# Eight instead of six of sixteen row tiles in seven products, and the MLP's pairs in another order

## The chip, the cores and the metric

The kernel runs on one core of a Trainium2 chip. The core has a matrix engine (TensorE, PE in the profile, with its weight loads as PEld), a vector engine (VectorE, DVE), a scalar engine (ScalarE, ACT), GpSimd (POOL) and a sync engine (SP) that issues most DMAs. Each engine works through its own instructions in order and waits for others by semaphores. The metric is the device time of one execution in microseconds.

## The reference

Two layers of a streaming encoder over 256 rows of 2048 columns, all in float32. Layer 1 is causal attention with forget gates over 16 heads, layer 2 attention in chunks of 64 with a learned bias on shared keys and values. Behind each attention stands the same MLP with its own weights, 2048 to 8192 to 2048; most of the work is there:

```
def sq_relu_mlp(h, g, w1, w2):
    a = jax.nn.relu(rms_norm(h, g) @ w1)
    return (a * a) @ w2
```

## The kernel before

**Products.** A float32 product is made of three passes on PE (lines 471, 473 and 475): each operand is split into a rounded high part and a low remainder, and high x high, high x low and low x high are summed. The weights come from HBM as tiles of 128 x 1024 (a *unit*: two row tiles of 512 columns), and `issue` (line 219) splits each: ACT writes `hi`, then DVE subtracts it from the tile and writes `lo`. Three `hi`/`lo` buffers of 1024 columns, and one of 512, let the splits run ahead of PE.

**Pairs.** A *pair* is two neighbouring panels of 512 output columns (a and b) over 16 row tiles, for both blocks of 128 rows. Of a part of the row tiles the products are made by Strassen's scheme: seven products in place of eight. The seven weight operands (*forms*) are, in order, 11, T3 = 22 + 12, T2 = T3 + 11, T1 = 12 + 11, 21, T4 = T2 + 21 and 22, where 11, 12, 21 and 22 are blocks of the weights. T3 and T2 are added on DVE (line 824); T1 and T4 are made by DMAs that POOL issues and that add a block from HBM onto a tile in place (line 830). On the side of the activations sums of row tiles stand against them (`S` for the MLP's input, `Sh` for a chunk of hidden columns), made and split in `sums`. A small pair uses four of its sixteen row tiles so, a wide one six: each form is then a unit of 1024 columns (f) and a half unit of 512 (h), with 2 + 1 products of three passes. The other row tiles are *own* units (a3 to a7, b3 to b7), each with four products of three passes. Of the 32 MLP pairs 30 are wide; the first of each MLP and the two pairs of the second layer's query are small.

**Order.** The MLP's 8192 hidden columns go in four chunks. A chunk has two pairs of the first matrix (four panels of hidden columns), then two pairs of the second matrix, which add to the residual. `plan_mlp` writes the order of all units out once, `Pair.plan` that inside a pair: forms, with own units between them, the last three of panel b (b5 to b7) among the first forms of the next pair. Every engine keeps the written order.

**Fill.** Everything else (turning a hidden panel, squaring, sums) is cut into steps in a list of slots. `run_fill` takes one slot after every own unit. A finished hidden panel is transposed in 32 x 32 blocks by DVE, written to DRAM and read back in four pieces by SP (`carry`), and `take` squares and splits it in the slots that a table names.

**Loads.** SP issues the own units' loads, three ahead. The wide blocks are brought by `bring` to rooms of 1536 columns, two each in the tags "k" and "v", at times that the tuple `units` counts in own units before the pair's start, as the adds of T3 and T1.

Of the kernel before, what the change touches and what calls it, by code (L numbers as in the profile page):

```python
# [9 lines left out]
F32 = mybir.dt.float32  # L10
# [5 lines left out]
P = 128  # L16
T = 256
# [11 lines left out]
AHEAD = 2  # L29
EARLY = 3  # L30
UA = UN // 512
REL = 384
WIDE = UN + 512
WIDE1 = (1, 2, 3, 4, 5, 6, 7)
# [15 lines left out]
def trunk(ctx: ExitStack, tc: tile.TileContext, xT, xr, gs, hg, bf, wgate, w_in, w_oa, w1a, w1fa, w1sa, w2fa, w2sa,  # L50
# [24 lines left out]
    def load_x(i):  # L75
        raw_x[i] = qkv.tile([P, WIDE], F32, name="xin", tag="kv"[i // 2], bufs=2)[:, : GH * T].rearrange("p (a t) -> p a t", a=GH)
        if i:
            SY.dma_start(raw_x[i], xT[:, i * GH : (i + 1) * GH, :])
# [40 lines left out]
    class Pair:  # L119
# [3 lines left out]
        def __init__(self, big, src, order, third, units, wide=False):  # L123
            self.big, self.src, self.third, self.units, self.order = big, src, third, units, order
            self.ps, self.t, self.adds, self.wide, self.own = None, {}, order != "early", wide, 3 if wide else 2
# [4 lines left out]
        def plan(self, rest):  # L130
            made = [self.items(f"f{i} h{i}" if self.wide else f"f{i}") for i in range(7)]
            own = {"early": "a2 F a3 F b2 F b3 a4 b4 a5 a6 a7", "wide": "a3 F b3 F a4 F b4 a5 a6 a7", "ahead": "a3 F a4 F a5 F a6 a7 b3 b4",
                   "query": "a2 F b2 F a3 F b3 a4 b4 a5 a6 a7", "": "a2 F a3 F a4 F a5 a6 a7 b2 b3 b4"}[self.order].split()
# [10 lines left out]
    def plan_mlp(w1, w1f, w1s, w2f, w2s, tail, more=None):  # L144
        pairs = []

        def add(w, wf, ws, i, wides, order, when):
            j = wides.index(i) if i in wides else i - sum(1 for k in wides if k < i)
            names = ("11", "12", "21", "22")
            if i in wides:  # L150
                src = [[None] * 3 + [ws[10 * j + 5 * q + u] for u in range(5)] for q in range(2)]
# [4 lines left out]
            pairs.append(Pair(big, src, order, len(pairs) % 2 == 0, when, i in wides))  # L156

        close = (7, 5, 1, 4, 3, 2)
        for c in range(NCH):
            for q in range(2):  # L160
                i = 2 * c + q
                order = "ahead" if i else "early"
                when = (25, 20, 9, 15, 10, 8) if not i else (9, 7, 1, 5, 3, 2) if i == 1 else close
                add(w1, w1f, w1s, i, WIDE1, order, when)
            for q in range(2):
                i = 2 * c + q
                add(None, w2f, w2s, i, WIDE2, "wide", close)
        if more is not None:
            for q in range(2):
                add(more, None, None, q, (), "" if q else "query", close)  # L170
# [910 lines left out]
```

## Time and profile before

| | |
|---|---|
| median of 3 runs | 2086.82 us (2086.47 to 2088.3) |
| span of the profiled execution | 2084.3 us |
| between span and median | 2.5 us |
| PE, DVE, ACT, POOL busy | 100%, 78%, 60%, 6% |
| granted PE clock | 1.00 |
| first MLP | about 350 to 1000 us |
| second MLP | about 1390 to 2080 us |

The profiled execution has no time of its own apart from its span; the median stands 2.5 us over it. A row of the groups view gives line, engine, operation, tiles and count, then the busy time and the mean of one in ns, then the idle time of the engine before them and what ended it. A row of the windows view gives the busy time of each engine in a stretch, the granted clock, the share of time that the 16 DMA engines were busy, and GB/s. A row of the DMA view gives the tiles, the issuing queue, the count, the size and the median time from issue to landing.

### The profile page before, as it was taken

What the parts mean: (1) busy time and instruction counts of PE and PEld (TensorE: products, weight loads), DVE (VectorE), ACT (ScalarE), POOL (GpSimd) and SP (SyncE); (2) the same over time, 40 slices, a digit from 0 to 9 for tenths busy, and PEclk for the clock granted to TensorE, in tenths of its full rate; (3) what the DMA queues carried; (4) which work ended last, traced back from release to release, by engine and by line L of the source; (5) the groups of instructions that cost most, each with busy time, mean ns of one, the idle gap of its engine ahead of it and who ended that gap; (6) DMA issues with size and microseconds to landing.
All of it is one profiled execution on the core that took longest, in us unless ns stands there. A gap on an engine that the chain in (4) does not pass through costs nothing.

```text
span 2084.3 us, 26346 instructions
## 1 busy us (share of the span) xinstructions
PE 2076.9 (100%) x9230; PEld 1721.4 (83%) x9230; DVE 1629.7 (78%) x1964; ACT 1256.1 (60%) x1637; POOL 118.4 (6%) x131
## 2 busy tenths in 40 slices
PE   9999999999999999999999999999999999999999
PEld 7888888888888888888878888888888888888887
DVE  6767666888788888788888677778987887888786
ACT  6544455766566566567676455456765665665664
POOL 1111000000000000000011001000000000000000
PEclk9999999999999999999999999999999999999999
DMA  7787788798798799789988777787987987988895
GB/s 288 247 257 243 225 258 265 253 276 277 235 286 270 251 278 298 217 276 294 269 244 276 225 239 234 244 265 265 282 264 254 278 272 241 289 271 250 271 288 165
DMA packets 181397, 540.93 MB, mean 260 GB/s; under 512 B 36864, under 2 KB 71568, under 8 KB 181264
## 3 DMA queue, kind: packets, MB, share of 16 engines
q1 hardware_dynamic: 170384, 483.60, 68.7%
q0 software_dynamic: 10592, 55.08, 14.3%
q8 instruction: 72, 1.18, 0.2%
q10 hardware_dynamic: 288, 0.57, 0.1%
q14 instruction: 61, 0.50, 0.1%
HBM read 499.30 MB, written 39.87 MB: 259 GB/s over the span
## 4 chain that ended last, share of the span: by engine, by line
PE 98%; DMA 1%; DVE 0%; ACT 0%; issue 0%; ACTq 0%; DVEq 0%; SPq 0%
PE acc L473 26%; PE acc L471 26%; PE acc L475 26%; PE s L471 6%; PE s L473 6%; PE s L475 6%; PE s L614 1%; PE po L644 1%; DMA w<-in_w2fa 0%; PE s L613 0%; PE po L645 0%; DMA raw<-in_w_in 0%; DVE lo L220 0%; ACT hi L219 0%; PE s L737 0%
## 5 line engine op out<-in xcount | busy, mean ns | idle before, releaser
L220 DVE TENSOR_TENSOR lo<-raw,hi 128x1024 fp32r<-128x1024 f32 (+1 forms) x574 | 695.5, 1215 | 219.5 <-ACT hi L219 203.6
L219 ACT ACTIVATE hi<-raw 128x1024 fp32r<-128x1024 f32 (+1 forms) x574 | 602.8, 1051 | 255.6 <-PE acc L473 194.8
L471 PE MATMUL acc<-hi,act 128*128 128x512 f32 x2108 | 580.3, 393 | 1.6 <-ACT hi L219 1.6
L473 PE MATMUL acc<-hi,act 128*128 128x512 f32 x2108 | 571.3, 389 | 0.1
L475 PE MATMUL acc<-lo,act 128*128 128x512 f32 x2108 | 570.9, 389 | 0.0
L473 PEld LDWEIGHTS acc<-hi,act 128*128 128x128 f32 x2108 | 395.5, 188 | 83.2 <-DVE act L311 0.7
L475 PEld LDWEIGHTS acc<-lo,act 128*128 128x128 f32 x2108 | 395.6, 188 | 82.2
L471 PEld LDWEIGHTS acc<-hi,act 128*128 128x128 f32 x2108 | 393.7, 188 | 81.5 <-ACT hi L219 1.7
L219 ACT ACTIVATE hi<-w 128x1024 fp32r<-128x1024 f32 x138 | 145.7, 1056 | 108.1 <-DMA w<-in_w1fa 25.1
L220 DVE TENSOR_TENSOR lo<-w,hi 128x1024 fp32r<-128x1024 f32 x138 | 167.5, 1214 | 27.4 <-ACT hi L219 25.0
L220 DVE TENSOR_TENSOR lo<-wT,hi 128x1024 fp32r<-128x1024 f32 x94 | 114.6, 1219 | 64.0 <-ACT hi L219 64.0
L219 ACT ACTIVATE hih<-w 128x512 fp32r<-128x512 f32 x120 | 75.2, 627 | 76.5 <-PE acc L473 65.5
L219 ACT ACTIVATE hi<-wT 128x1024 fp32r<-128x1024 f32 x94 | 99.1, 1055 | 27.7 <-PE acc L473 9.1
L471 PE MATMUL s<-hi,act 128*128 128x512 f32 x386 | 104.6, 389 | 0.0
L475 PE MATMUL s<-lo,act 128*128 128x512 f32 x386 | 104.6, 389 | 0.0
L473 PE MATMUL s<-hi,act 128*128 128x512 f32 x386 | 104.6, 389 | 0.0
L219 ACT ACTIVATE hih<-wT 128x512 fp32r<-128x512 f32 x90 | 56.4, 627 | 72.9 <-PE acc L473 63.2
L220 DVE TENSOR_TENSOR loh<-w,hih 128x512 fp32r<-128x512 f32 x120 | 82.3, 686 | 18.9 <-ACT hih L219 18.8
L473 PEld LDWEIGHTS s<-hi,act 128*128 128x128 f32 x386 | 72.5, 188 | 15.1
L475 PEld LDWEIGHTS s<-lo,act 128*128 128x128 f32 x386 | 72.5, 188 | 15.0
L471 PEld LDWEIGHTS s<-hi,act 128*128 128x128 f32 x386 | 72.4, 188 | 15.0
L220 DVE TENSOR_TENSOR loh<-wT,hih 128x512 fp32r<-128x512 f32 x90 | 62.0, 689 | 21.0 <-ACT hih L219 20.7
(220 smaller groups left out, 1961.4 us busy)
## 6 DMA issues: line engine op xcount, KB each, us to landing
raw<-in_w_in SPq DMA_DIRECT2D x95, 512.0 KB, 4.5
raw<-in_w2sa SPq DMA_DIRECT2D x80, 512.0 KB, 5.8
raw<-in_w2sb SPq DMA_DIRECT2D x80, 512.0 KB, 5.8
raw<-in_w1sa SPq DMA_DIRECT2D x70, 512.0 KB, 6.0
raw<-in_w1sb SPq DMA_DIRECT2D x70, 512.0 KB, 6.0
raw<-in_w_kv SPq DMA_DIRECT2D x64, 512.0 KB, 4.5
turn<-z SPq DMA_DIRECT2D x60, 512.0 KB, 4.2
w<-in_w2fa SPq DMA_DIRECT2D x32, 768.0 KB, 7.4
```

The costliest lines, as they stand in the source:

```text
L219: S.activation(hi[:, c], raw[:, c], AF.Copy)
L220: V.tensor_tensor(lo[:, c], raw[:, c], hi[:, c].bitcast(F32), op=ALU.subtract)
L471: TE.matmul(ps[:, cols], xh, cut(hi, j), start=first, stop=False, **kw)
L473: TE.matmul(ps[:, cols], xl, cut(hi, j), start=False, stop=False, **kw)
L475: TE.matmul(ps[:, cols], xh, cut(lo, j), start=False, stop=last, **kw)
L614: TE.matmul(s[:, P : 3 * P], q[:, a, P:T], k[:, a], start=True, stop=True)
L644: TE.matmul(po[:, :T], v[:, 0, a * P : (a + 1) * P], pT[:, :2], start=True, stop=False)
```

## The change

- The thirty wide pairs become *deep*: eight of sixteen row tiles go through the seven forms. A form is two units of 1024 columns (f and h), each with two products of three passes; eight own units remain (a4 to a7, b4 to b7). T3 and T2 are added in two halves. The half-width `hi`/`lo` buffers are no longer used by them.
- Four rooms of 2048 columns (k0, k1, v0, v1), one buffer each, take the blocks; each pair passes them on in rotation. The accumulating DMAs are 1024 KB. The scratch for POOL's descriptors is set to 2048 bytes.
- The order of the pairs is new: between the two second-matrix pairs of a chunk, and behind them, stands one first-matrix pair of the next chunk.
- A slot of fill also follows every second unit of a form (`run_fill` in the branch of the forms), and `fetch` is called for each unit of a form.
- Most hidden panels hop: `hop` moves 16 blocks of 32 partitions by DMA from the transposed tile straight to the other tile, eight issued by SP and eight by POOL. In each MLP three of sixteen, the second panel of chunks 1 to 3, still go by `carry`. The tables of slots and times are new.
- `S` and `Sh` hold sums of eight row tiles; tiles in the pool "p" are 4096 instead of 3456 columns.

```diff
+    "deep0": "a4 F F b4 a5 F a6 a7",
+    "deep1": "a4 F b4 F F a5 a6 a7",
+    "ahead0": "F a4 F a5 a6 a7 F b4",
+    "ahead1": "a4 F a5 F a6 a7 F b4",
...
+UNITS = {
+    "W1I1": (9, 7, 6, 5, 4, 1),
+    "W1F": (6, 5, 1, 4, 4, 1),
+    "W1S": (6, 5, 2, 4, 4, 3),
+    "W2F": (7, 5, 1, 5, 4, 3),
+    "W2S": (8, 8, 3, 4, 3, 2),
+    "W2L": (6, 6, 1, 3, 3, 1),
...
+TURNS = (
+    ((1, -1, 4, 5, 6, 6, 6, 9, 9),
+     (0, -1, 3, 5, 7, 7, 8, 9, 9),
+     (1, -1, 5, 7, 7, 7),
+     (1, -1, 3, 4, 5, 5)),
+    ((0, -1, 4, 14, 14, 14, 14, 19, 19),
+     (0, 3, 7, 10, 10, 13, 16, 18, 19),
+     (1, -1, 4, 6, 7, 7),
+     (0, -1, 4, 5, 5, 5)),
+)
...
+DEEP = 2 * UN
...
+        rooms = {"12": "v0", "22": "k0", "11": "k1", "21": "v1"}
+        seq = [(0, 0, 0), (0, 0, 1)]
         for c in range(NCH):
+            seq += [(1, c, 0)] + [(0, c + 1, 0)] * (c + 1 < NCH) + [(1, c, 1)] + [(0, c + 1, 1)] * (c + 1 < NCH)
...
+            p.rooms = rooms
+            if p.adds:
+                rooms = {"12": rooms["11"], "22": rooms["12"], "11": rooms["21"], "21": rooms["22"]}
...
-        if form and half == form.pair.wide:
+        if form and form.pair.deep and form.name == "T3":
+            make(form.pair, "T2", int(half))
+        elif form and half == form.pair.wide:
...
     def room(tag, name, dtype=F32):
-        return qkv.tile([P, WIDE], dtype, name=name, tag=tag, bufs=1 if tag == "bias" else 2)
+        return qkv.tile([P, DEEP], dtype, name=name, tag=tag, bufs=1)
...
+    def hop(z, dst):
+        n = z.shape[1] // 4
+
+        def go():
+            for i in range(4):
+                for j in range(4):
+                    (G if i % 2 else SY).dma_start(dst[32 * j : 32 * j + 32, i * n : (i + 1) * n], z[32 * i : 32 * i + 32, j * n : (j + 1) * n])
+
+        return [[go], [], [], [], []]
...
-    def form_products(ps, hi, lo, x, fs, i, half, stop):
+    def form_products(ps, hi, lo, x, fs, i, half, p):
         items = []
-        for g in (2,) if half else range(2):
+        groups = p.cols // 512
+        for g in range(2, groups) if half else range(2):
...
+        p.t[name] = room(p.rooms[name], "w" + name)
+        SY.dma_start(p.t[name][:, : p.cols], p.big[name])
...
-        G.dma_start(p.t[name][:, : WIDE if p.wide else UN], p.big[other], accum_op=ALU.add)
+        G.dma_start(p.t[name][:, : p.cols], p.big[other], accum_op=ALU.add)
...
     def prepare(p, d):
+        if p.deep and d == p.units[4] - 1:
+            make(p, "T3", 1)
...
-            hi, lo = ready.popleft()[:2] if q > 1 and ready else fetch()
+            hi, lo = ready.popleft()[:2] if q > 1 and ready and not p.deep else fetch()
...
-                    top_up(AHEAD - 1)
+                    if not p.deep:
+                        top_up(AHEAD - 1)
                     if u == 1:
                         S.activation(p.ps[1][0], p.ps[1][1], AF.Copy, scale=-1.0)
+                    if p.deep:
+                        run_fill()
...
-    nc = bacc.Bacc("TRN2", target_bir_lowering=False, num_devices=1)
+    nc = bacc.Bacc("TRN2", target_bir_lowering=False, num_devices=1, dynamic_dma_scratch_size=2048)
```

More of the change, by code (lines that the diff above doesn't have):

```diff
@@ L121, in trunk, with __init__ @@
         fast = True
[L123 to L125 removed]
+        def __init__(self, big, src, order, third, units, wide=UN):
+            self.big, self.src, self.third, self.units = big, src, third, units
+            self.ps, self.t, self.adds, self.order = None, {}, order != "early", order
+            self.deep, self.wide = wide == DEEP, wide > UN
+            self.cols, self.own = wide, wide // 512
         def items(self, names):
@@ L131, in plan @@
             made = [self.items(f"f{i} h{i}" if self.wide else f"f{i}") for i in range(7)]
-            own = {"early": "a2 F a3 F b2 F b3 a4 b4 a5 a6 a7", "wide": "a3 F b3 F a4 F b4 a5 a6 a7", "ahead": "a3 F a4 F a5 F a6 a7 b3 b4",
-                   "query": "a2 F b2 F a3 F b3 a4 b4 a5 a6 a7", "": "a2 F a3 F a4 F a5 a6 a7 b2 b3 b4"}[self.order].split()
+            own = ORDERS[self.order].split()
             plan = made[0] + rest[:1] + made[1] + rest[1:2] + made[2] + rest[2:] + made[3]
@@ L211, in issue @@
             form, half = raw, raw.half
-            raw, cuts = form.pair.t[form.name], [slice(0, 512 if half else UN)]
+            raw, cuts = form.pair.t[form.name], [slice(0, form.pair.cols - UN if half else UN)]
             if half:
@@ L229, in half_next @@
         u = raws[0][0] if raws else units[0]
-        return isinstance(u, Form) and u.half
+        return isinstance(u, Form) and u.half and not u.pair.deep
     def top_up(ahead=AHEAD, early=EARLY):
```

118 lines of the change are left out of this document (63 added, 55 removed), and 3 rows, old and new, of the table ORDERS.

## The prediction

> **What bounds the kernel now.** I read the page first: busy shares, slices, the chain.
>
> ```profile
> span 2084.3 us, 26346 instructions
> PE 2076.9 (100%) x9230; PEld 1721.4 (83%) x9230; DVE 1629.7 (78%) x1964; ACT 1256.1 (60%) x1637; POOL 118.4 (6%) x131
> PE 98%; DMA 1%; DVE 0%; ACT 0%; issue 0%; ACTq 0%; DVEq 0%; SPq 0%
> ```
>
> PE is idle for 7.4 us of 2084.3, and the chain is PE for 98%. What counts is the number of matmuls and whether the other engines still deliver in time. The profiled execution spans 2084.3 us; the median of the runs is 2086.8 us, so 2.5 us lie around the span. I apply differences to the median.
>
> Next the stretches of one pair (about 41 us) by engine, then PE's timeline in plain units, where four matmuls of one pass stand on a line.
>
> ```profile
> 618.00:659.00 41.00, 41.00 (x183) 33.95 (x182) 35.70 (x40) 28.66 (x34) 1.71 (x2) 1.00 0.97 296
> 659.00:700.00 41.00, 41.00 (x183) 33.96 (x182) 32.62 (x34) 22.81 (x27) 1.71 (x2) 1.00 0.77 235
> sum 409.00, PE 409.00 PEld 338.78 DVE 338.02 ACT 262.89 POOL 16.19; mean PE 40.90 PEld 33.88 DVE 33.80 ACT 26.29 POOL 1.62
> 618.00:645.00 27.00, 27.00 (x121) 22.37 (x120) 25.17 (x31) 19.26 (x25) 1.71 (x2) 1.00 0.95 268
> ...
> 944.96 1.07 PE L473 MATMUL acc<-hi,act 128*128 128x512 f32 x4
> 954.02 1.07 PE L475 MATMUL acc<-lo,act 128*128 128x512 f32 x4
> ```
>
> The columns after the stretch are PE, PEld, DVE, ACT and POOL busy, the granted clock (1.00), the DMA share and GB/s; the third row covers ten such stretches (415 to 824 us). PE never waits here. DVE is at 33.8 of 40.9 us, ACT at 26.3. The DMA share swings: 0.97 where hidden panels are turned, 0.77 where only weights move. From 944.96 to 954.02 ten groups of four start, so a matmul costs PE 9.06 / 40 = 0.2265 us.
>
> **The change, part by part.**
>
> *Matmuls removed.* A wide pair issues per form (2 + 1) products of 3 passes, 7 forms: 63 matmuls, and 10 own units of 12: 183. After it, 7 x 4 x 3 = 84 and 8 units of 12: 180. Thirty pairs lose 90 matmuls: 90 x 0.2265 = 20.4 us on the path. A pair then lasts 180 x 0.2265 = 40.8 us, a half form 1.36 us, an own unit 2.72 us.
>
> *Splits and adds.*
>
> ```profile
> L220 DVE TENSOR_TENSOR lo<-raw,hi 128x1024 fp32r<-128x1024 f32 x570 | 692.9, 1219 | 218.5 <-ACT hi L219 202.6 <-PE acc L473 9.3 <-DMA raw<-in_w2sa 1.1
> L219 ACT ACTIVATE hi<-raw 128x1024 fp32r<-128x1024 f32 x570 | 600.5, 1054 | 254.7 <-PE acc L473 194.8 <-PE s L473 18.3 <-DMA raw<-in_w_in 14.0
> L220 DVE TENSOR_TENSOR loh<-w,hih 128x512 fp32r<-128x512 f32 x120 | 82.3, 686 | 18.9 <-ACT hih L219 18.8
> L219 ACT ACTIVATE hih<-w 128x512 fp32r<-128x512 f32 x120 | 75.2, 627 | 76.5 <-PE acc L473 65.5 <-PE s L473 9.9
> L824 DVE TENSOR_TENSOR wT<-wT,w 128x1536 f32<-128x1536 f32 x30 | 52.8, 1759 | 1.0
> L824 DVE TENSOR_TENSOR wT<-w,w 128x1536 f32<-128x1536 f32 x30 | 52.0, 1734 | 0.0
> L296 DVE TENSOR_TENSOR Sh<-sum,Sh 128x512 fp32r<-128x512 f32 x24 | 15.7, 683 | 0.0
> ```
>
> Per pair: full splits go from 17 to 22, half-width ones from 7 to none, and T3 and T2 become two adds of 1024 columns each, which I price like a split. DVE: +5 x 1.219 - 7 x 0.686 - 1.759 - 1.734 + 4 x 1.219 = +2.7 us. ACT: 5 x 1.054 - 7 x 0.627 = +0.9 us, covered by over 10 us idle a pair. The second hidden panel's sums are now full-width: one more low split (0.683) and wider adds, an estimate of 1.3 us a chunk, 0.3 us a pair. DVE's 33.8 of 40.9 becomes 34.2 + 2.7 + 0.3 = 37.2 of 40.8 us, 91% on average. Pairs that handle the first two hidden panels stand higher: 35.7 + 2.7 + 0.6 = 39.0, or 96%. The fourth row of the windows above is the cover: 27 us with DVE busy for 25.17 (93%) and PE never waiting. If 93% were DVE's ceiling, 39.0 would need 41.8 us: 1.0 us of stall in each of 16 such pairs, 16 us. If its gaps there are mere slack, the cost is nothing. I take 4 us, nearer nothing, since the new order puts a second-matrix pair between the heavy ones and single wide adds no longer hold the queue for 1.76 us.
>
> *Lookahead.* Forms are now two equal units of 1.36 us through the three-deep hi/lo buffers. A split starts when PE leaves the hi pass of the unit three back, some 4 us before its low half is needed; ACT and DVE together take 1.05 + 1.22 us plus a hand-over. About 1.5 us of slack remains, which one add of 1.22 us fits. Cost nothing while DVE isn't behind.
>
> *DMA.*
>
> ```profile
> q1 hardware_dynamic: 170384, 483.60, 68.7%
> q0 software_dynamic: 10592, 55.08, 14.3%
> raw<-in_w2sa SPq DMA_DIRECT2D x80, 512.0 KB, 5.8
> turn<-z SPq DMA_DIRECT2D x60, 512.0 KB, 4.2
> w<-in_w2fa SPq DMA_DIRECT2D x32, 768.0 KB, 7.4
> q<-turn SPq DMA_DIRECT2D x168, 128.0 KB, 5.5
> w<-in_w1fa POOLq DMA_DIRECT2D x7, 768.0 KB, 9.7
> wT<-in_w2fb POOLq DMA_DIRECT2D x8, 768.0 KB, 7.8
> pbuf<-turn SPq DMA_DIRECT2D x128, 48.0 KB, 2.8
> query<-in_w_qb POOLq DMA_DIRECT2D x2, 512.0 KB, 5.9
> query<-turn POOLq DMA_DIRECT2D x4, 128.0 KB, 5.2
> L347 POOL DMA_DIRECT2D query<-turn x4: 552/568/612, 1063.7 to 1065.4; - x4
> L347 SPq DMA_DIRECT2D q<-turn x168: 325/426/1282, 345.9 to 2012.6; - x168
> L331 DVE STREAM_TRANSPOSE z<-acc 128x512 f32<-128x512 f32 x48 | 31.4, 692 | 5.1 <-PE acc L475 5.1
> ```
>
> Weights read by plain loads stay 8 MB a pair (4 x 768 + 10 x 512 KB against 4 x 1024 + 8 x 512). Only the two accumulating loads of a pair (T1, T4) grow by a third. Sixty of them are 47 of the queue's 55 MB, so about 12% of 16 engines' span, 4.2 us each, now 5.7: +2.9 us a pair. Turning a panel raises the share by 0.20 over two pairs of 82 us for four panels, 4.1 us of all engines each; 26 of 32 panels now hop from SBUF to SBUF without the write to DRAM. A hop costs between half of that and all of it. Four pairs with four turns then come to (0.77 x 164 + 4 x 2.9 + 10 to 16) / 163 = 0.91 to 0.94 throughout. That is below the 0.97 which PE bears today without waiting, and it no longer swings.
>
> *Queues.* Each hop puts 8 issues on SP and 8 on POOL. On POOL that is 8 x 0.57 = 4.6 us, ahead of which the next pair's T1 may stand and behind which nothing urgent does, T4 having gone before. From the end of the panel: transposes 1.3 us (two of 0.69 us, overlapping), 7 x 0.57 = 4.0 us, landing 5.2 us: 10.5 us. The squared ReLU is asked for four slots on, 10.9 us later. For the last panel of a chunk it is asked for after 8 to 9.5 us, up to 2.5 us early; ACT then waits with two units in hand, mostly an own unit. I take 1 us for all hops; nothing and 8 x 2.5 = 20 us are the ends, and the spare units point to the lower.
>
> *Rooms.* Each wide load now has one room, passed on from pair to pair. Block 22 can be fetched only once T1 of the pair before is split: T1's second half is a unit at 17.7 us, split nearly two units ahead, done at an estimated 15.4 us; where SP first writes out a panel, 18 us. From 512 to 768 KB the landing grows by 1.6 us, so 1 MB takes about 9.0 us and lands at 24.4 to 27.0; T3 is asked for behind the own unit at 24.5 us, so near 25.9 at the earliest. DVE may wait 1.1 us, in front of own units or forms with as much slack. Nothing to 1.1 x 8 = 9 us; I take 0, as every other transition has 1.5 us or more.
>
> *The end and the start* keep their order (the last two second-matrix pairs still follow each other). Nothing.
>
> **Sum:** 2086.8 - 20.4 + 4 + 1 + 0 = 2071.4 us.
>
> **Rivals.**
>
> *T4 lands late: the slower one.* T4 adds block 21 from HBM into T2's room. POOL must wait until T2 is split, then the load runs, and its result is due at the sixth form.
>
> ```profile
> 671.57 0.60 ACT L908 ACTIVATE p<-acc 128x512 f32<-128x512 f32 x1 [3.40 <-PE acc L475]
> 673.01 0.59 ACT L914 ACTIVATE acc<-acc 128x512 f32<-128x512 f32 x1
> 675.27 0.86 POOL L830 DMA_DIRECT2D wT<-in_w2fa  x1 [13.02 <-DVE loh L220]
> POOL wT L830 <- DVE loh L220: 360.4, 29, 14.2
> ```
>
> ACT stands in front of this split until PE ends the second form (8.2 us into the pair); two copies of 0.6 us and the split (1.05 + 1.22 us) put T2's last low half at 11.8 us. In 14 pairs (orders "deep0" and "ahead0") the sixth form's split must start by 23.3 us: 11.5 us for the load. In the other 16 one more own unit lies between: 14.2 us. From 5.9 us (512 KB) and 7.8 us (768 KB) the new one takes 9.7 us, 10.4 in proportion: in time by over a us. But the slowest accumulating row, 9.7 us, in proportion gives 12.9 us, and the gain is gone (14 x 1.4 = 20 us). It decides for slower from 13.3 us (14 x 1.8 = 25 us); at 14 us the time is 2086.8 - 20.4 + 35 = 2101 us. Against it: the 9.7 us row is T1's, issued among many loads, T4's rows are the lower ones, and POOL holds nothing before it.
>
> *DVE is the bound.* At the 93% ceiling above: 16 us in place of 4, and with up to 9 us of late T3 the time is 2082 to 2091 us. It needs heavy pairs to stand 1.5 us over (above 3.3 us of forced gaps a pair) to end slower.
>
> *Small pieces are served one by one.* If a group of four short pieces (2.8 us and three further issues of some 0.42 us, 4.1 us) had to end before the next began, the 16 pieces of a hop would take 16.4 us, 5.5 us beyond the slots; with 1.5 us covered, 26 x 4 = 104 us, or 2170 us. Against it: four 128 KB pieces, in total as much as a hop, land 5.2 to 5.5 us after issue though issued on top of each other. The Trainium skill, DMA: Bandwidth & Descriptors, section Bandwidth, says that transfers under 64 KB are descriptor-dominated and gives 0.95 us for 64 KB and 0.68 us for 4 KB; at an estimate of 0.8 us by that page, sixteen in a row take 13 us, with the transposes 3.4 us late, and 26 x (3.4 - 1.5) = 49 us give 2120 us. The trace's overlapping pieces speak against a plain sum of that kind. No run here shows a 32 KB piece between two SBUF tiles.
>
> **Chances.** The forecast (stalls of 0 to 10 us, 2066 to 2077 us): 0.58. Half the gain eaten by DVE or by T3's waits (2077 to 2082.6): 0.12. Gain and stalls cancel, within 4.2 us, the 0.2% that a measurement can tell: 0.10. Slower 0.20: T4 0.11, hops 0.05, DVE 0.04. So faster 0.70, same 0.10, slower 0.20. The range starts at the full gain and a us beyond, 2065, and ends at 2092 us, which leaves the slower cases out.
>
> **What would show it.** Right: 512-column splits gone, full splits of w and wT 120 and 90 higher, those of raw 60 lower; PE with about 9140 matmuls and still 99% or more; DVE near 37 of 40.8 us; DMA share even, 0.90 to 0.95; accumulating rows near 9 to 10.5 us. Wrong: PE idle in front of forms released by DVE (DVE bound), ACT waiting over 2 us for wT loads (T4) or for q after a hop; more than 20 us of PE idle in all makes the prediction wrong.

## The result, and the profile after

The changed kernel takes 2090.07 us (median of 17 runs, 2084.96 to 2097.05) against 2087.31 us for the kernel before in the same job (17 runs, 2085.26 to 2089.75): a ratio of 1.0014, 95% interval 1.0006 to 1.0022. It is slower by 0.14%, inside the 0.2% that was taken for no change, where a gain of 0.7% was forecast. The forecast was 18.7 us too low; the time lies inside its range.

The page of the profile after the change (span and busy shares, POOL's DMA queue, chain, issues with KB and median us to landing; the last three rows are of the DMA view):

```profile
span 2088.3 us, 26874 instructions
PE 2068.8 (99%) x9140; PEld 1703.1 (82%) x9140; DVE 1710.9 (82%) x1974; ACT 1313.2 (63%) x1587; POOL 224.7 (11%) x339
...
q0 software_dynamic: 17248, 77.64, 18.7%
...
PE 76%; issue 10%; DMA 10%; DVE 3%; ACT 1%; POOL 0%; SPq 0%; ACTq 0%; DVEq 0%; POOLq 0%
wT<-in_w2fa POOLq DMA_DIRECT2D x8, 1024.0 KB, 10.6
q<-z SPq DMA_DIRECT2D x208, 32.0 KB, 5.6
q<-z POOLq DMA_DIRECT2D x208, 32.0 KB, 5.8
```

PE has the 9140 matmuls that the change promised, 90 fewer, yet the chain is PE for only 76%, not 98%. The 4.0 us by which the profiled span grew (2088.3 against 2084.3) split up from the two pages: 90 matmuls fewer, -20.4 us; PE idle for 2088.3 - 2068.8 = 19.5 us in place of 7.4, +12.1 us; and PE busy for 2068.8 us where 2076.9 - 20.4 = 2056.5 would do, +12.3 us. The last is not more work but the same matmuls, taking longer. One stall of the first chunk shows how PE comes to wait. The timelines of POOL, SP, ScalarE (ACT) and PE around it (start, duration, operation, count, and in brackets the idle time before it and what ended that):

```profile
473.85 0.92 POOL L882 DMA_DIRECT2D wT<-in_w2fa  x1 [8.60 <-DVE lo L257]
480.71 3.46 POOL L395 DMA_DIRECT2D q<-z  x7 [5.94 <-DMA w<-in_w1fa]
487.53 0.50 POOL L395 DMA_DIRECT2D q<-z  x1 [3.35 <-DMA q<-z]
...
480.44 7.52 SPq L395 DMA_DIRECT2D q<-z  x8
488.08 0.51 SPq L860 DMA_DIRECT2D w<-in_w1fa  x1
...
487.36 2.00 ACT L256 ACTIVATE hi<-wT 128x1024 fp32r<-128x1024 f32 x2 [6.02 <-DMA wT<-in_w2fa]
...
488.46 0.99 PE L519 MATMUL acc<-hi,act 128*128 128x512 f32 x2 [2.34 <-ACT hi L256]
489.25 1.06 PE L521 MATMUL acc<-hi,act 128*128 128x512 f32 x2
490.11 1.06 PE L523 MATMUL acc<-lo,act 128*128 128x512 f32 x2
```

T4, the load that adds block 21 into T2's room, is issued at 473.85. ScalarE asks for its sum from 481.3 on, waits 6.02 us, gets it at 487.36, and PE stands for 2.34 us. In between a hop is under way: SP needs 7.52 us to issue its eight pieces (the fastest of the 26 hops takes 4.9 us), and POOL gives out seven and must wait 3.35 us for a landing before the eighth. SP's next weight load, at 488.08, stands behind that. The rows of the tile give T4's own landing here and in the same place two chunks later, the next two are POOL's timeline there, and the last shows the granted clock behind the stall (the column ahead of the DMA share):

```profile
DMA to landing us min/median/max: 13.4/13.4/13.4
DMA to landing us min/median/max: 11.6/11.6/11.6
...
808.45 0.92 POOL L882 DMA_DIRECT2D wT<-in_w2fa  x1 [9.42 <-DVE lo L257]
820.30 0.50 POOL L395 DMA_DIRECT2D q<-z  x1 [2.03 <-DMA wT<-in_w2fa]
...
488.80:492.10 3.30, 3.30 (x9) 2.58 (x8) 3.30 (x4) 3.26 (x4) 0.00 (x0) 0.50 0.91 298
```

T4 took 13.4 us here and 11.6 us two chunks later. What POOL's eighth piece waits for can be worked out from these rows: T4 lands at 473.85 + 13.4 = 487.25, and the piece starts at 487.53, 0.28 us later; in the other place T4 lands at 808.45 + 11.6 = 820.05, and the piece starts at 820.30. So it waits for T4, although nothing in the data asks for that. The operands of the issues say why: each names a semaphore that its landing raises, SP and ScalarE take eight of them in turn (100, 102, 104, 105, 106, 108, 109 and 110), POOL eight others (111 to 118), and an issue waits until the transfer issued eight before it has landed. Eight back from a hop's eighth piece on POOL stands the adding load that was issued ahead of the hop. SP's eighth piece, at 487.45, waits in the same way for a weight load issued at 475.07.

Behind the stall PE runs at half its clock: 0.50 is granted from 488.8 to 492.1, and the last two lines of PE's timeline, two matmuls each, start 0.86 us apart, 0.43 us a matmul rather than 0.2265. The trace has this stretch as 3.41 us long, so it costs 1.7 us. The Trainium skill, TensorE: Matmul & The Clock Gate, Part 1, says that the clock halves after an idle window of about 3.4 us; here a stand of 2.34 us came before it, and the page's half rate agrees with the granted 0.50.

Half clock explains only a part of the 12.3 us. The trace has one more such stretch inside the run, 7.5 to 10.9 us, behind the start; the two cost 3.4 us. The other 9 us pass at full clock. The view counts a line as busy until about 0.39 us after its last matmul starts (two last 0.62 us, four 1.07), while the next could start after 0.2265 us, so up to 0.16 us of every delay counts as busy. By the starts in the two traces such hidden delays come to 19.1 us at full clock, before to 10.4.

Over the whole run these are the waits for arriving data that ScalarE and POOL show (total us, times, longest):

```profile
ACT hi L256 <- DMA wT<-in_w2fa: 19.7, 6, 6.0
ACT hi L256 <- DMA wT<-in_w2fb: 8.7, 3, 4.2
ACT q L899 <- DMA q<-z: 5.4, 4, 2.0
POOL q L395 <- DMA q<-z: 28.1, 11, 4.1
```

The first two are the accumulating loads of the second matrix, 28.4 us over 9 waits. The third is the squared ReLU that asks for a panel before it has landed. The fourth is new in kind: pieces of a hop held on POOL. The view names the landing it saw last, here a piece; by the operands five of these waits, 18.4 of the 28.1 us, are for T1 or T4 as in the first place above, and six are for an earlier piece of the same hop, where T1 was issued between the pieces. Further holds by T1 and T4 stand in rows under their own names.

### The profile page after: what moved, and what is told of

The parts are those of the page before. It is cut to its first block, busy times and chain, and to the rows that moved or that the text cites. A ratio compares the mean times of both kernels' runs of the same rounds, so it can differ in the third digit from the quotient of the medians.

```text
span 2088.3 us, 26874 instructions
## 1 busy us (share of the span) xinstructions
PE 2068.8 (99%) x9140; PEld 1703.1 (82%) x9140; DVE 1710.9 (82%) x1974; ACT 1313.2 (63%) x1587; POOL 224.7 (11%) x339
## 3 DMA queue, kind: packets, MB, share of 16 engines
q0 software_dynamic: 17248, 77.64, 18.7%
## 4 chain that ended last, share of the span: by engine, by line
PE 76%; issue 10%; DMA 10%; DVE 3%; ACT 1%; POOL 0%; SPq 0%; ACTq 0%; DVEq 0%; POOLq 0%
PE acc L523 21%; PE acc L519 20%; PE acc L521 20%; PE s L523 4%; PE s L519 4%; PE s L521 4%; DVE lo L257 2%; DMA w<-in_w2fa 1%; DMA wT<-in_w2fa 1%; DMA turn<-z 1%; DMA wT<-in_w2fb 1%; ACT hi L256 1%; DMA w<-in_w2fb 1%; DMA w<-in_w1fb 1%; DMA raw<-in_w2sa 1%
## 5 line engine op out<-in xcount | busy, mean ns | idle before, releaser
L256 ACT ACTIVATE hi<-raw 128x1024 fp32r<-128x1024 f32 (+1 forms) x514 | 540.4, 1054 | 344.6 <-PE acc L521 257.6
L257 DVE TENSOR_TENSOR lo<-raw,hi 128x1024 fp32r<-128x1024 f32 (+1 forms) x514 | 618.6, 1212 | 165.0 <-ACT hi L256 150.0
L256 ACT ACTIVATE hi<-w 128x1024 fp32r<-128x1024 f32 x258 | 270.7, 1057 | 109.0 <-PE acc L521 68.2
L257 DVE TENSOR_TENSOR lo<-w,hi 128x1024 fp32r<-128x1024 f32 x258 | 310.1, 1219 | 18.9 <-ACT hi L256 17.7
L257 DVE TENSOR_TENSOR lo<-wT,hi 128x1024 fp32r<-128x1024 f32 x184 | 222.2, 1221 | 74.9 <-ACT hi L256 73.6
L256 ACT ACTIVATE hi<-wT 128x1024 fp32r<-128x1024 f32 x184 | 192.9, 1058 | 110.6 <-PE acc L521 35.6
L395 POOL DMA_DIRECT2D q<-z x208 | 105.6, 547 | 266.5 <-DVE z L369 127.2
L876 DVE TENSOR_TENSOR wT<-w,w 128x1024 f32<-128x1024 f32 x62 | 75.4, 1217 | 7.9 <-DMA w<-in_w1fb 2.7
L876 DVE TENSOR_TENSOR wT<-wT,w 128x1024 f32<-128x1024 f32 x62 | 76.0, 1225 | 2.1
L605 POOL TENSOR_TENSOR ss<-ss,mhalf 128x4 f32<-128x4 f32 x32 | 43.3, 1360 | 273.0 <-DVE ss L604 272.8
```

Source lines behind the costliest of these rows:

```text
L256: S.activation(hi[:, c], raw[:, c], AF.Copy)
L257: V.tensor_tensor(lo[:, c], raw[:, c], hi[:, c].bitcast(F32), op=ALU.subtract)
L395: (G if i % 2 else SY).dma_start(dst[32 * j : 32 * j + 32, i * n : (i + 1) * n], z[32 * i : 32 * i + 32, j * n : (j + 1) * n])
L605: G.tensor_tensor(rn, vv, mhalf, op=ALU.pow)
L876: V.tensor_tensor(d, a, b, op=ALU.add)
```

## The experiments

Four theories stood at the start: T4 lands late (first rival of the prediction); DVE has become the bound (second); the hop of sixteen small pieces holds the queues and delays what is behind them; and, as a part of the last, that the crossing of partitions matters. Each kernel was timed against the kernel before in its own job, whose median lay between 2086.7 and 2087.7 us. The short diffs are against the changed kernel unless another is named.

**The change again**, with no edit:

> The changed kernel unaltered, as the yardstick of this chip. All theories: 2085 to 2095 us, with PE stalls of 15 to 25 us inside the two MLPs. Two of the stalls of its first trace are single events (2.1 us at the start, 4.3 us near 486 us, each with matmuls at half speed behind a long idle); if they are chance they stand elsewhere or are missing here.

2093.1 us (2088.5 to 2102.85), ratio 1.0032 (1.0016 to 1.0048). It spreads by 14 us where the kernel before spreads by 5: what it waits for is near its due time, and small shifts decide. Differences of 3 us between variants of this kind carry no weight below.

**T4 in two halves.** The first half is issued as soon as T2's first half has been split.

```
+        elif form and form.pair.deep and form.name == "T2":
+            put(form.pair, "T4", int(half))
-        G.dma_start(p.t[name][:, : p.cols], p.big[other], accum_op=ALU.add)
+        c = slice(0, p.cols) if half is None else slice(half * UN, half * UN + UN)
+        G.dma_start(p.t[name][:, c], p.big[other][:, c], accum_op=ALU.add)
```

> T4's adding load is issued in two halves, the first as soon as the first half of T2 is split. T4 theory (T4 lands after its 11.5 us in the pairs behind a chunk's last hidden panel, some 12 of the 20 us of stalls): 8 to 12 us faster than the changed kernel, no wait of ScalarE for wT over 1 us. DVE theory (VectorE at over 90% delays low halves): within 3 us of the changed kernel, since VectorE's work stays. Pieces theory (a hop's 16 DMAs are more than the queues hold in flight, so SP's loads and POOL's last piece wait): within 3 us, or slower, as POOL has one DMA more in flight.

2083.82 us, ratio 0.9986 (0.9976 to 0.9995): 6 to 9 us of the loss are T4's, as the T4 theory expected, though waits of up to 2.9 us for its sums remain. The waits for second-matrix sums fall from 28.4 us to 10.7, but those of the squared ReLU for its panel rise from 5.4 to 13.4. Something else stands behind T4.

**A later use of T4.** Two orders of products give T4 one more unit of time.

```
-    "deep0": "a4 F F b4 a5 F a6 a7",
+    "deep0": "a4 F b4 F F a5 a6 a7",
-    "ahead0": "F a4 F a5 a6 a7 F b4",
+    "ahead0": "a4 F a5 F a6 a7 F b4",
```

> The sixth form is moved behind one more own unit in the 14 pairs with the short window, so T4 has 14.2 instead of 11.5 us; nothing else moves. T4 theory: 6 to 10 us faster than the changed kernel, the waits for wT shrink by about 2.7 us each. DVE theory and pieces theory: within 3 us.

2108.83 us, ratio 1.0103 (1.0088 to 1.0118), slower still, where 6 to 10 us of gain were expected. The moved own units ask earlier for plain loads from SP, and these are late (below the row of the waits SP's timeline and ScalarE's in one of six like places):

```profile
ACT hi L256 <- DMA raw<-in_w1sb: 13.6, 3, 5.0
...
679.52 9.24 SPq L860 DMA_DIRECT2D w<-in_w2fa  x2
688.81 2.52 SPq L239 DMA_DIRECT2D raw<-in_w1sa  x4
...
697.36 1.06 ACT L256 ACTIVATE hi<-raw 128x1024 fp32r<-128x1024 f32 x1 [5.15 <-DMA raw<-in_w1sa]
```

The own units' loads stand on SP behind the second of two 1 MB block loads, which went out only at 688.4, and no hop lies ahead of them. Time given to T4 is time taken from these loads; of the hop this run tells nothing. The next three kernels change the hop alone.

**A hop in four pieces** of 128 partitions (128 KB each), two per queue; the exchange between groups of partitions is left out:

```
-                for j in range(4):
-                    (G if i % 2 else SY).dma_start(dst[32 * j : 32 * j + 32, i * n : (i + 1) * n], z[32 * i : 32 * i + 32, j * n : (j + 1) * n])
+                (G if i % 2 else SY).dma_start(dst[:, i * n : (i + 1) * n], z[:, i * n : (i + 1) * n])
```

> A hop moves the same bytes in the same rows of 1 KB, but in 4 pieces of 128 partitions instead of 16 of 32; the exchange between groups of partitions is left out. Pieces theory: SP's issues take under 2 us a hop instead of 5 to 7.5, loads are on time, 6 to 12 us faster than the changed kernel. T4 theory by bytes alone: the waits for wT stay, within 4 us. DVE theory: within 3 us.

2073.14 us, ratio 0.9934 (0.9919 to 0.9949). With the same bytes and the same work on every compute engine, 17 to 20 us come back, more than the 6 to 12 expected. The stretch from 415 to 1000 us, some fourteen pairs, after the change and with four pieces, with one double pair of the latter below it (PE, PEld, DVE, ACT, POOL busy, clock, DMA share, GB/s):

```profile
415.00:1000.00 585.00, 578.09 (x2526) 473.90 (x2526) 517.92 (x517) 397.66 (x416) 76.84 (x132) 1.00 0.87 268
```

```profile
415.00:1000.00 585.00, 584.71 (x2569) 481.24 (x2569) 528.60 (x527) 403.80 (x425) 39.87 (x55) 1.00 0.88 273
...
418.00:500.00 82.00, 81.86 (x357) 66.26 (x356) 79.31 (x82) 61.75 (x67) 8.88 (x13) 1.00 0.87 267
```

DVE is *busier* with four pieces, 528.60 us of 585 (36.9 of 40.8 us a pair) against 517.92, and PE gets 2569 matmuls done in the same time rather than 2526: 43 x 0.2265 = 9.7 us. In the stretch with the most for it to do DVE is at 79.31 of 82 us, 97%, and PE at 81.86: beside a DVE at 97% PE is idle for 0.14 us. As the cause of the loss the second rival has fallen; a kernel below, with T4 in halves as well, shows PE without a gap beside a DVE as busy.

**Eight pieces** of 64 partitions, the exchange left out as well, and **sixteen that don't cross** partitions:

```
-                for j in range(4):
+                for j in range(2):
-                    (G if i % 2 else SY).dma_start(dst[32 * j : 32 * j + 32, i * n : (i + 1) * n], z[32 * i : 32 * i + 32, j * n : (j + 1) * n])
+                    (G if i % 2 else SY).dma_start(dst[64 * j : 64 * j + 64, i * n : (i + 1) * n], z[64 * j : 64 * j + 64, i * n : (i + 1) * n])
```

```
-                    (G if i % 2 else SY).dma_start(dst[32 * j : 32 * j + 32, i * n : (i + 1) * n], z[32 * i : 32 * i + 32, j * n : (j + 1) * n])
+                    (G if i % 2 else SY).dma_start(dst[32 * j : 32 * j + 32, i * n : (i + 1) * n], z[32 * j : 32 * j + 32, i * n : (i + 1) * n])
```

> A hop in 8 pieces of 64 partitions, 4 on SP and 4 on POOL, the same bytes in the same rows of 1 KB; the exchange between groups of partitions is left out. Pieces theory in its narrow form (each queue holds eight DMAs in flight, and the ninth waits for an old one): four pieces mostly fit, so like hop_few, 2072 to 2077 us. If each piece costs by itself: halfway, about 2080. T4 theory by bytes: as the changed kernel, over 2088.

> A hop in 16 pieces of 32 partitions as in the changed kernel, but each piece stays on its own partitions; the exchange is left out. Pieces theory: the number counts and not the exchange, so as the changed kernel, 2088 to 2095 us. If crossing between groups of partitions is what costs: as hop_few, 2072 to 2077.

2081.23 us (ratio 0.9971, 0.9959 to 0.9982) and 2094.66 us (1.0039, 1.0025 to 1.0054). Four, eight and sixteen pieces give 2073, 2081 and 2095 us for the same 512 KB. Sixteen that stay in their partitions cost as much as sixteen that cross: the number counts, not the crossing. The narrow form of the pieces theory, by which only a ninth transfer in flight costs, expected 2072 to 2077 us of the eight and missed: POOL's pieces are never held there and SP gives out its four in 2.4 us (at 808.33), yet ScalarE waits 27.7 us over 11 times for second-matrix sums, as much as after the change, against 19.4 us over 8 with four pieces (one profile of each). So a held queue isn't all that pieces cost.

**No hop at all:** every hidden panel by way of DRAM, read back on POOL; and the same with T4 in halves (diff as above).

```
-                    way = [hop(*zt)[0][0]] if at[1] < 0 else [i[0] for i in carry(*zt, 0)[:2]]
+                    way = [hop(*zt)[0][0]] if at[1] < 0 else [i[0] for i in carry(*zt, 0, G)[:2]]
```

> No hop: every hidden panel is written to DRAM by one DMA of SP and read back by four of POOL, which waits for the write in SP's place; slots of the last panel and of the second of chunk 0 moved two later. The full result. Pieces theory: SP is free, four to six DMAs in flight on POOL, so 2072 to 2080 us although the DMA engines carry more bytes. T4 theory by bytes: T4 shares the engines with more traffic, no better than the changed kernel, 2088 or more.

> As carry_pool, and T4's adding load in two halves. If late T4 still costs anything once the pieces are gone, 2 to 5 us faster than carry_pool; if T4's late landing was only the pieces' doing, within 2 us of it.

2182.96 and 2186.85 us (ratios 1.0458, 1.0442 to 1.0475, and 1.0486, 1.0446 to 1.0526), where 2072 to 2080 were expected of the first. The table of slots was also moved so that the reading comes after the writing, but not far enough:

```profile
ACT q L899 <- DMA q<-turn: 92.5, 22, 9.4
POOL q L385 <- DMA turn<-z: 308.6, 30, 14.3
```

The panels land up to 9.4 us after the squared ReLU asks, and POOL stands 308.6 us for the write to DRAM, T1 and T4 behind it. This tells nothing of the hop; it shows what late panels are worth, 90 us and more.

**The hop in the kernel before**, in place of its way through DRAM (against that kernel, with the same function `hop`):

```
-                    add_fill(carry(*zt, 0)[:2] + [[step] * uses.count(i) for i in range(3, uses[-1] + 1)])
+                    add_fill(hop(*zt) + [[step] * uses.count(i) for i in range(3, uses[-1] + 1)])
```

> The kernel before with one part of the change alone: its hidden panels hop in 16 pieces instead of going through DRAM; six of sixteen row tiles, the old order and the old slots stay. Pieces theory: SP is held 5 to 7 us a hop in place of about 3 with the way through DRAM, its loads and POOL's adding loads come later; with two rooms a block and windows of 12 us for T4 some of it is covered: 3 to 15 us slower than before, with stalls of PE where it had none. If a hop costs nothing of its own and only the deep pairs' narrow windows make it dear: within 2 us of before.

2088.46 us, ratio 1.0003 (0.9994 to 1.0012): no difference, where the pieces theory expected 3 to 15 us. There, with loads of 768 KB in that order of work, POOL's pieces are hardly held (its waits have no row for pieces), and a hop leaves SP in 5.0 us in the median rather than 7.1. A hop isn't dear by itself, but in the deep pairs' surroundings; whether by the larger loads, the narrower windows or the fuller DVE, this run can't tell.

**Twelve pieces.** The four blocks on the diagonal don't leave their partitions. ScalarE copies them, right before its ReLU; then the same with T4 in halves.

```
+                    if i != j:
                         (G if i % 2 else SY).dma_start(dst[32 * j : 32 * j + 32, i * n : (i + 1) * n], z[32 * i : 32 * i + 32, j * n : (j + 1) * n])
...
+            for i in range(4 if z is not None else 0):
+                d = slice(32 * i, 32 * i + 32), slice(i * T, i * T + T)
+                S.activation(t[d], z[d], AF.Copy)
```

> The four blocks of a hop that keep their place are copied by ScalarE (four copies of 32 x 256 ahead of the ReLU), so a hop has 12 DMAs, 6 a queue. The full result. Pieces theory: between 8 pieces (2081) and 16 (2093 to 2095), 2084 to 2089 us, SP held about 4 us a hop. If ScalarE's 1.7 us a panel matter: as the changed kernel or slower.

> As hop_twelve, and T4's adding load in two halves. Where both causes add, 2076 to 2081 us, faster than either kernel with the full result; if they are the same stalls seen twice, as t4_halves (2084).

2103.45 us (1.0067, 1.0054 to 1.0079) and 2096.4 us (1.0038, 1.0025 to 1.005): worse than both ranges of the theory of pieces, and at first sight against it. The timelines of ScalarE and PE in one of twelve like places show another cause:

```profile
551.79 1.68 ACT L902 ACTIVATE q<-z 32x256 f32<-32x256 f32 x4
553.50 1.06 ACT L903 ACTIVATE q<-q 128x1024 f32<-128x1024 f32 x1
554.46 1.04 ACT L256 ACTIVATE hi<-wT 128x1024 fp32r<-128x1024 f32 x1
...
555.55 0.73 PE L520 MATMUL s<-hi,Sh 128*128 128x512 f32 x2 [0.85 <-ACT hi L256]
```

Four block copies (1.68 us), the ReLU and only then the split that PE needs: 0.85 us of idle PE each time, and late starts behind it at full clock (1.00 in this run). That looks like a fault of the place, so the copies were given a slot of their own, ahead of the ReLU's.

**A hop in four pieces with T4 in halves** (both diffs above) says how much is to be had:

> A hop in 4 pieces (the exchange left out) and T4 in two halves: what is left when both are out of the way. T4 theory: the remaining waits for wT (31 us on ScalarE, some 5 us on PE) go, 2067 to 2071 us. DVE theory for the rest: no change from hop_few, 2072 to 2075.

2070.38 us, ratio 0.9914 (0.9901 to 0.9928). That lies in the range of the T4 theory. With the queues free, T4 early and the exchange left out, the time is that of the forecast, 2071.4. The stretch of the first MLP has DVE at 531.00 us of 585 and PE without a gap:

```profile
415.00:1000.00 585.00, 585.00 (x2580) 483.69 (x2579) 531.00 (x527) 407.49 (x428) 53.59 (x70) 1.00 0.89 273
```

So neither DVE nor the total of the DMA engines bounds the deep pairs there.

**Twelve pieces, the copies in an earlier slot, T4 in halves:**

```
+        def keep(z, dst):
+            for i in range(4):
+                d = slice(32 * i, 32 * i + 32), slice(i * T, i * T + T)
+                S.activation(dst[d], z[d], AF.Copy)
...
+                    if at[1] < 0:
+                        items[2 if n % 2 == 0 or at[0] else 1].append(lambda: keep(*zt))
```

> Full result. Twelve crossing pieces (6 on SP, 6 on POOL), the four diagonal blocks copied by ScalarE in a slot of their own two units ahead of the squared ReLU, and T4 in halves. In hop_twelve twelve regular stalls of 1.46 us stood where the copies and the ReLU shared one slot, 15.5 us in each whole run of the sums by region. Theory (a held queue grows with the number of pieces, and the copies cost only by their place): those stalls go, 2076 to 2081 us, below the kernel before at 2087. Rival (the copies themselves cost ScalarE's lead wherever they stand): 2090 us or more, as hop_twelve_halves with 2096.

2074.17 us (2071.61 to 2078.36), ratio 0.9939 (0.9928 to 0.9951): faster than both kernels, with the full result, by 12.6 us against before in its job, and 2 us below the range that the theory gave. The page, and the two queues where the stall stood:

```profile
span 2072.2 us, 26810 instructions
PE 2063.0 (100%) x9140; PEld 1702.6 (82%) x9140; DVE 1714.1 (83%) x1974; ACT 1354.6 (65%) x1691; POOL 225.9 (11%) x317
...
469.92 0.92 POOL L886 DMA_DIRECT2D wT<-in_w2fa  x1 [12.15 <-DVE lo L257]
477.93 3.00 POOL L398 DMA_DIRECT2D q<-z  x6 [5.99 <-DVE z L371]
...
477.66 4.57 SPq L398 DMA_DIRECT2D q<-z  x6
```

POOL issues its six pieces without a stop, 3.00 us, and nowhere in this run are its pieces held. SP needs 4.57 us for its six rather than 7.52 for eight. PE is idle for 9.2 us in all.

**Which queue?** With the exchange left out, one queue keeps eight small pieces and the other gets two large ones. For SP with two (the mirror for POOL):

```
+                if i % 2:
+                    for j in range(4):
+                        G.dma_start(dst[32 * j : 32 * j + 32, i * n : (i + 1) * n], z[32 * j : 32 * j + 32, i * n : (i + 1) * n])
+                else:
+                    SY.dma_start(dst[:, i * n : (i + 1) * n], z[:, i * n : (i + 1) * n])
```

> The exchange of blocks between partitions is left out, so what the hidden panels hold is not the transposed panel. SP moves its half of a hop in 2 pieces of 128 KB, POOL its half in 8 pieces of 32 KB: ten pieces in all, as many as in pool_few. Theory (SP held by its own hop lets its weight loads start late): SP is held some 1 us in place of 7.0, time near that of hop_few, 2073 to 2078 us. Rival A (POOL's last piece, standing behind T4 and T1, is what costs): 2086 to 2094 us, near hop_straight's 2095. Rival B (each piece costs time in the DMA engines, whoever issues it): between eight pieces (2081) and sixteen (2095), 2082 to 2085 us, the same as pool_few.

> The mirror of sp_few, the exchange left out likewise: SP moves its half of a hop in 8 pieces of 32 KB, POOL its half in 2 pieces of 128 KB. Theory (SP held): SP stays held for about 7 us, time 2086 to 2094 us, near hop_straight's 2095. Rival A (POOL's pieces behind T4 and T1): 2073 to 2078 us. Rival B (a cost for each piece in the DMA engines): 2082 to 2085 us, the same as sp_few.

2089.57 us (1.0011, 1.0002 to 1.002) and 2087.5 us (0.9999, 0.9988 to 1.0009). The first came out as rival A expected and the second as the theory did, and these two deny each other; rival B alone expected both alike, but lower. Either queue's eight pieces by themselves cost most of what both queues' do. The waits say that they do it in two ways:

```profile
POOL q L396 <- DMA q<-z: 26.5, 13, 3.5
ACT q L902 <- DMA q<-z: 25.1, 18, 2.4
...
545.54 0.50 POOL L396 DMA_DIRECT2D q<-z  x1 [2.03 <-DMA q<-z]
554.34 1.06 ACT L902 ACTIVATE q<-q 128x1024 f32<-128x1024 f32 x1 [1.67 <-DMA q<-z]
```

```profile
ACT hi L256 <- DMA wT<-in_w2fa: 17.9, 6, 5.3
ACT hi L256 <- DMA wT<-in_w2fb: 17.8, 6, 4.9
...
808.45 6.66 SPq L396 DMA_DIRECT2D q<-z  x8
DMA to landing us min/median/max: 11.8/11.8/11.8
```

With eight on POOL (the first fence), its last piece is held until 545.54 by earlier landings, and the squared ReLU waits for the panel, 18 times, 25.1 us. With eight on SP (the second), hardly a panel is late (3.4 us in all), but SP needs 6.66 us for its eight, T4 issued at 802.6 lands 11.8 us later, and ScalarE waits 35.7 us over 12 times for such sums. With two pieces on each queue the same T4 needs 10.3 us:

```profile
DMA to landing us min/median/max: 10.3/10.3/10.3
```

Over four kernels the waits for these sums go with the pieces on SP and not with POOL's: 19.4 us with two on each queue, 20.3 with two on SP and eight on POOL, 27.7 with four on each, 35.7 with eight on SP and two on POOL. A T4 that has a hop beside it lands after 9.8, 9.7, 10.3 and 11.0 us in the mean of eight. If there are two ways, halves of T4 must cure the second and not the first:

> The exchange is left out as in pool_few (SP 8 pieces of 32 KB, POOL 2 of 128 KB), and T4 comes in halves. In pool_few ScalarE waits 35.7 us over 12 times for the accumulating second-matrix loads, the longest 5.3 us, and hardly for a panel (3.4 us). Theory (with POOL's pieces few, all that is left is T4 landing late): the halves bring nearly all back, 2071 to 2075 us. Rival (SP held by its eight pieces costs by itself): 2080 to 2086 us.

> The exchange is left out as in sp_few (SP 2 pieces of 128 KB, POOL 8 of 32 KB), and T4 comes in halves. In sp_few ScalarE waits 25.1 us over 18 times for a panel, whose last piece stands on POOL behind a T1 load, and 20.3 us for accumulating second-matrix loads. Theory (two costs, one for each queue): the halves take only the second away, 2078 to 2084 us. Rival (one cost, T4 late): 2071 to 2075 us as pool_few_halves.

2076.02 us (0.9945, 0.9933 to 0.9956) and 2087.76 us (1.0001, 0.9992 to 1.0011). They do, the first 1 us and the second 4 us above what was expected of it. With two pieces on POOL the halves bring 11.5 us; with eight they bring 1.8, though the waits for second-matrix sums fall there too, from 20.3 to 4.9 us; the panels have become the later of the two:

```profile
ACT q L905 <- DMA q<-z: 29.0, 19, 3.1
```

```profile
ACT q L905 <- DMA q<-z: 3.2, 3, 1.7
```

**Three queues.** All sixteen pieces, six on SP, six on POOL and the four diagonal ones on ScalarE's queue, T4 in halves (against the twelve pieces with early copies):

```
-                S.activation(dst[d], z[d], AF.Copy)
+                S.dma_start(dst[d], z[d])
...
-                        items[2 if n % 2 == 0 or at[0] else 1].append(lambda: keep(*zt))
+                        items[1].append(lambda: keep(*zt))
```

> Full result. Sixteen crossing pieces as in the change, but the four diagonal ones are issued by ScalarE's queue, so that SP and POOL issue six each; T4 in halves. Theory (a queue is held when it issues more pieces than it may have in flight): 2074 to 2078 us, as twelve_early_halves (2074.2), though all sixteen pieces pass through the DMA engines. Rival (the load of sixteen pieces on the DMA engines costs, whoever issues them): 2081 to 2085 us, as t4_halves (2083.8). If issuing costs ScalarE more than its four copies did, stalls stand behind ScalarE in the trace and neither follows.

2130.02 us, ratio 1.0205 (1.0192 to 1.0218): neither the theory's number nor the rival's, but the case named last. The hold moved onto ScalarE itself:

```profile
ACT hi L256 <- DMA q<-z: 91.9, 17, 7.9
...
632.21 8.00 ACTq L929 DMA_DIRECT2D q<-z  x4
631.95 7.51 SPq L398 DMA_DIRECT2D q<-z  x6
632.21 3.00 POOL L398 DMA_DIRECT2D q<-z  x6 [1.38 <-DVE z L371]
```

ScalarE takes 8.00 us to give out four pieces, waiting for landings before the later ones, and its splits stand behind them: 91.9 us over 17 waits. SP is held again, 7.51 us for six pieces, while POOL's six take 3.00 us. In the operands of these issues SP and ScalarE wait on the same eight semaphores of landings, POOL on eight others. So the rotation of eight is one for SP and ScalarE together and another for POOL, and a third queue doesn't widen it. The engines' load as such stays untested by this run.

## Why the prediction was wrong, point by point

*Matmuls removed*: right. 9140 matmuls, and with the hop cheap and T4 halved 17.3 of the 20.4 us show (2070.38 against 2087.72 us before in that job, a ratio of 0.9914).

*Splits and adds*: the sum was right, the fear behind its range was not. DVE's busy time rose by 1710.9 - 1629.7 = 81.2 us, 2.7 a pair where 3.0 was worked out, and with the queues free it runs at 36.9 of 40.8 us with PE served. The 4 us taken for DVE stalls came out near the whole loss of the best variant, 20.4 - 17.3 = 3.1 us, by luck: no run puts that rest down to DVE. ACT was put 0.9 us a pair up and went up by 1313.2 - 1256.1 = 57.1 us, 1.9 a pair; it is covered, as said.

*Lookahead* and *Rooms*, each set to nothing: the adds of T3 wait 5.2 us for blocks in the whole run, 5 times, 2.1 us the longest, so a little was there; the late rows that the experiments move are T4's and the panels'.

*DMA*: half right. POOL's queue went from 14.3% of 2084.3 us to 18.7% of 2088.3, 92 us or 3.1 us a pair where 2.9 was said of the accumulating loads alone; its half of the hops is in it. The share over 585 us is 0.87, not 0.91 to 0.94. Four pieces get more done at 0.88, so the total was not the limit.

*Queues*: **the step that failed.** It priced a hop as issue time, "8 x 0.57 = 4.6 us" on POOL "behind which nothing urgent does", 10.5 us to the landing, and took 1 us for all hops of a range of 0 to 20. The trace has a hop on SP at 7.1 us in the median, 4.9 at best, and POOL's eighth piece 6.8 us after its first (480.71 to 487.53) rather than 4.0; even unheld a piece takes SP 0.6 us, not 0.42. "T4 having gone before" was taken for an advantage; it is what holds the eighth piece, which may not go out before T4 has landed. The prediction counted instructions and not what may be outstanding, and it gave the pieces no effect on T4, which is late with SP's pieces beside it. That SP's own loads come late behind a hop is not seen to cost: of the loads that ScalarE waits for in the two MLPs only two, 1.6 us of waits, were issued within 4 us behind one. The runs put this term at 17 to 20 us (the change at 2090 to 2093 against four pieces at 2073), the upper end of its own range. T4's lateness beside the pieces is in that sum.

*T4 lands late*, the first rival: half true. The medians of its rows, 10.6 and 9.9 us, are what was worked out (9.7 to 10.4), and two of the three late ones, 11.6, 12.1 and 13.4 us, sit where a hop of eight pieces on SP runs beside it (with two on POOL such a T4 takes 11.8 us, with two on each queue 10.3). Against this rival the prediction had said that POOL holds nothing before T4; it did not look at what starts after it. Halving T4 alone gave back 6 to 9 us. The costs of the two queues don't add up: either alone is worth 14 to 16 us (2087.5 and 2089.6 against 2073.1), both together 17 to 21.5 (2094.7 without the exchange). A PE that stands for a panel gives T4 time, which may be the reason; no run tests it.

*Small pieces are served one by one*: not so. A piece lands 5.6 to 5.8 us after its issue in the median, with up to sixteen under way; only the issue of the last ones is late. Nor is each free: in the stall above the sixteen land one after another from 487.6 to 490.1, some 0.17 us apart, all behind T4. The section Bandwidth of the page DMA: Bandwidth & Descriptors in the Trainium skill, weighed there, calls transfers under 64 KB dominated by their descriptors; its sum, 2120 us, was not met, but four pieces of 128 KB did beat sixteen of 32 KB by 17 to 20 us.

*What would show it*: the counts of splits and matmuls came as listed; "more than 20 us of PE idle in all makes the prediction wrong" stands at 19.5 us in the profiled run. The sentence counted idle time alone and missed that as much again, 12.3 us, would pass as busy time: 3.4 us in two stretches at half clock, the rest in delays too short to show as idle.

What stays open: why T4 takes 1.5 us longer beside eight pieces on SP than beside two of the same total size, and why POOL's pieces don't do that to it; that SP is held can't be the whole reason, as some of it shows with four pieces that aren't held. Open is also the start of the kernel, where the profiled run lost some 2 us in the first 25 us that the profile of the same code in another job did not lose: a longer first wait (2.62 us) and the stretch at half clock behind it.

## What to carry to other kernels

Count, for each queue, not only the issues that a moved step adds but how many transfers may be in flight when they come: past that number an issue waits for a landing, and all behind it on the engine waits too. Look which transfer stands that many back: a slow load there holds a piece that has nothing to do with it. Cut a transfer into no more pieces than its access pattern forces, keep on the spot what needn't travel, and give it a slot of its own on an engine with time. A load with a due time can often start in halves, as soon as the first half of its room is free. And add up where PE's starts come late, not only its idle time.

## What the runs showed of the hardware

An issue in this program waits until the transfer eight before it in its set has landed; SP and ScalarE share one set of eight semaphores, POOL has its own. POOL's held pieces start 0.28 us behind that landing. Six or fewer pieces on POOL were never held (the kernels with four, eight and twelve pieces); with eight, the waits view has 11 to 13 such waits in the changed kernel and each variant that kept eight there. That semaphores are waited for by the issuing engine, and not by the DMA engines, is what the Trainium skill says too (DMA: Bandwidth & Descriptors, Anatomy of one DMA); the eight are this program's choice, seen in its operands. A piece of 32 KB between two SBUF tiles lands in 5.6 to 5.8 us, one of 128 KB in 6.2 to 7.0 us: under this load the size hardly counts. An accumulating load of 1 MB from HBM takes 9.0 to 10.6 us in the median. A stand of PE of 2.34 us was followed by 3.41 us at 0.50 of the clock; a stand of 2.20 us in the second run of the change too (0.51 from 653.5 to 656.9 us). The twelve stands of 0.85 us with twelve pieces were not.
